# Four modulation vectors as row products on VectorE instead of matmuls on TensorE

## The chip, the cores and the metric

One core of a Trainium2 chip runs the whole program in one launch. The metric is the device time of an execution in microseconds (us), lower is better. Its engines are named as the profile names them: PE (TensorE, matmuls), PEld (its weight loads), DVE (VectorE), ACT (ScalarE), POOL (GpSimd, which here mostly issues DMAs) and SP (SyncE, which issues most loads). Each engine works through its own list of instructions in the order in which the list was built; a wait holds everything behind it on that engine.

## The reference, cut to what matters

Two blocks run one after the other on 512 tokens of width 1024, with 256 context tokens. Block 1 is a mixer of three branches (retention, banded window attention, neighbourhood attention) and a routed FFN. Six vectors of 1024, the modulation, scale and shift its activations:

```python
sc = jax.nn.silu(c)                                    # c: 1024 numbers
mod_x = (sc @ w_mod + b_mod).reshape(-1, 6, d)         # w_mod: 1024 x 6144
hx = modulate(rms_norm(x, g_mix), mod_x[:, 0], mod_x[:, 1])
hc = modulate(rms_norm(ctx, g_mix), mod_c[:, 0], mod_c[:, 1])
mx, mc = hybrid_mixer(hx, hc, w_in, ...)               # retention, window, neighbourhood
x = x + mod_x[:, 2, None] * mx
hx = modulate(rms_norm(x, g_ffn), mod_x[:, 3], mod_x[:, 4])
x = x + mod_x[:, 5, None] * expert_choice_ffn(hx, ...)
```

The first two vectors are needed at once; the last four (`mod_x[:, 2]` to `mod_x[:, 5]`, 4096 numbers out of a 1024 x 4096 matrix, 16 MB) only when the mixer is done. Block 2 (two layers of latent attention, pooled attention and gated linear attention) has modulation vectors of its own for each layer, from the matrices `mw0a`, `mw0b`, `mw1a`, `mw1b`.

## The kernel before

Activations lie transposed, features on the partitions, in tiles of 128 x 512 tokens. A projection streams one 128 x 1024 piece of the weight (`wr`, 512 KB, SP's queue), ACT casts it (`wh`, L395), DVE takes the rest of the split (`wl`, L391), and PE multiplies three products per k-chunk (L404, L405, L406); eight k-chunks fill one PSUM tile `ps`. Three PSUM tiles serve the projections (tag `mm`), so a projection waits until the one three before it has been read.

A modulation vector is computed by `modblock` (L460 to L488): a tile `wm` of 128 x 1024 (512 KB) is loaded on SP's queue into one of `nbig` buffers (tag `wbig`, 3 here), and two matmuls of 512 columns (L471) multiply it with the silu of `c`, spread over 32 columns; the trace counts each as two records. Eight k-chunks accumulate four strips in a PSUM bank; ACT copies them out (L477), four transposes (L480) put them on the partitions, and DVE adds the bias (L486).

`block1_mixer` (L1090) is in stages. Its retention stage (L1111 to L1133) computes two pairs of retention heads: `ret_proj(0)`, `ret_proj(1)` are projections, `ret_attn(0)`, `ret_attn(1)` the attention, with `weave` putting other work between the steps of one. The list `mods` holds four generators: `modblock` for `wmod1` and `wmod2` (16 tiles each, block 1's last four vectors), `mods2` and `mods2g` (`mw1a` and `mw1b`, 24 tiles, block 2's second layer). `pace` (L282) hands out one step of `mods` for so much other work, the numbers of `PACE`. The context's normalised activations `hc` are built in the same stage. The window stage follows: its key is projected, turned by the rope tables `cosw` and `sinw` (lines L721 to L727, DVE; the tables are loaded by POOL), stacked (`kw`, and the context's keys `cw`), then the queries likewise (`qf`, `qw`), and the first scores are L940.

Instructions are listed by a scheduler that orders each engine's list from costs it assumes; what is wrapped in `late` keeps its place in the program's order relative to the others so wrapped and is not moved forward.

Of the kernel before, what the change touches and what calls it, by code (L numbers as in the profile page):

```python
# [7 lines left out]
F32 = mybir.dt.float32  # L8
# [7 lines left out]
D = 1024  # L16
# [127 lines left out]
def prep(i):  # L144
    f = {k: np.asarray(v) for k, v in i.items()}
    o = dict(_constants())
    o["xT"] = _tokT(f["x"][0])
    o["cT"] = _tokT(f["ctx"][0])
    o["cc"] = np.ascontiguousarray(np.stack([_cols(f["c"][0]), _cols(f["c_ctx"])], axis=-1))
    m = _modchunks(f["w_mod"][0])  # L150
    for n, a in enumerate(m):
        o[f"wmod{n}"] = a
    o["bmod"] = _cols(f["b_mod"][0])
    o["gmix"] = _cols(f["g_mix"][0])
    o["gffn"] = _cols(f["g_ffn"][0])
    o["gfin"] = _cols(f["g_final"])
    w = f["w_in"][0]
    off = {}
    at = 0
    for n, s in (("q_r", 512), ("k_r", 512), ("v_r", 512), ("g_r", 512), ("q_w", 512), ("k_w", 128), ("v_w", 128),  # L160
                 ("q_n", 512), ("k_n", 512), ("v_n", 512), ("gates", 3072)):
        off[n] = (at, s)
        at += s
    order = []

    def cols(n, a, m):
        return w[:, off[n][0] + a:off[n][0] + a + m]

    for h in (0, 256):
        order += [_tiles(cols(n, h, 256)) for n in ("q_r", "k_r")]  # L170
        order += [_vtiles(cols("v_r", h, 256)), _tiles(cols("g_r", h, 256))]
    order += [_tiles(cols("k_w", 0, 256)), _tiles(cols("q_w", 0, 512))]
    for h in (0, 256):
        order += [_tiles(np.concatenate([cols("q_n", h, 128), cols("k_n", h, 128)], axis=1)),
                  _vtiles(cols("v_n", h, 256)),
                  _tiles(np.concatenate([cols("q_n", h + 128, 128), cols("k_n", h + 128, 128)], axis=1))]
    order.append(_tiles(cols("gates", 0, 3072)))
    o["win"] = np.concatenate(order)
    o["lgt"] = _bcast(f["ret_decay_logit"][0])
    o["gn"] = _cols(f["ret_gn"][0])  # L180
    o["sink"] = _bcast(f["win_sink"][0])
    o["wbr"] = np.concatenate([_tiles(f["w_ret"][0]), _tiles(f["w_win"][0]), _tiles(f["w_na"][0])])
    o["wout"] = _tiles(f["w_out"][0])
    o["wrt"] = np.concatenate([f["w_router"][0], np.zeros((D, 16), np.float32)], axis=1).reshape(8, 128, 32).transpose(1, 0, 2)

    wg, wu, wd = [f[n][0].reshape(8, 2, 2, 4, 128, 2, 512).transpose(0, 5, 2, 1, 4, 3, 6)
                  for n in ("w_exp_gate", "w_exp_up", "w_exp_down")]
    o["wexp"] = np.concatenate([np.stack([wg, wu], axis=2).reshape(8, 16, 128, 2048), wd.reshape(8, 8, 128, 2048)],
                               axis=1)
    idx, ok = _na_index()  # L190
    rpb = f["na_rpb"][0]
    o["nab"] = np.stack([np.where(g[None], rpb[:, a[0], a[1]], np.float32(NEG)) for a, g in zip(idx, ok)], axis=1)
    _prep2(f, o)
    return {k: np.ascontiguousarray(v) for k, v in o.items()}
# [40 lines left out]
def drain(g):  # L235

    while True:
        try:
            next(g)
        except StopIteration as e:  # L240
            return e.value
# [40 lines left out]
def pace(main, extra, every):  # L282

    due = 0.0
    for c in main:
        yield c
        due += c
        while due >= every:
            due -= every
            c = next(extra, None)  # L290
            if c is not None:
                yield c
# [25 lines left out]
class Kern:  # L318
# [141 lines left out]
    def modblock(s, sc, src, width, dst, bias, col0, big=None, ps=None):  # L460

        nc = s.nc
        ps = s.mm() if ps is None else ps
        nj = width // 512
        for k in range(8):
            for j in range(nj):
                if j % 2 == 0:
                    w = s.wp.tile([128, 1024], F32, name=s.uid("wr"), tag="wraw", bufs=NRAW) if big is None else \
                        big.tile([128, 1024], F32, name=s.uid("wm"), tag="wbig", bufs=s.nbig)
                    nc.sync.dma_start(w, src[k][:, j * 512:j * 512 + 1024])  # L470
                nc.tensor.matmul(ps[32 * j:32 * j + 32, :], sc[:, k, :], w[:, j % 2 * 512:j % 2 * 512 + 512],  # L471
                                 start=k == 0, stop=k == 7)
                if j % 2:
                    yield 0.9
        n = 32 * nj
        rows = s.T(nm="mrow", tag="t5")
        nc.scalar.copy(rows[:n], ps[:n])  # L477
        pt = s.at()
        for i in range(4):
            nc.tensor.transpose(pt[:, i * 128:i * 128 + n], rows[:n, i * 128:i * 128 + 128],  # L480
                                s.const("ident")[:n, :n])
        pv = pt.rearrange("p (i j v) -> p j i v", i=4, j=4)
        for v in range(2):
            o = dst[:, v, col0:col0 + 4 * nj].rearrange("p (j i) -> p j i", j=nj)
            b = bias[:, col0:col0 + 4 * nj].rearrange("p (j i) -> p j i", j=nj)
            nc.vector.tensor_tensor(o, pv[:, 0:nj, :, v], b, ALU.add)  # L486
        yield 0.5


    def rstd_c(s, sq_sum, n, width, fold=None):  # L490
# [599 lines left out]
    def block1_mixer(s, xd, M, ctx2):  # L1090
# [18 lines left out]
        R = [{}, {}]  # L1109
        Y = []  # L1110
        with s.pool("rp") as s.rp, s.pool("mr") as mr:  # L1111
            s.nbig = 3
            pm = s.sc()
            bk = [pm[:, i * 512:i * 512 + 512] for i in range(3)]
            mods = itertools.chain(s.modblock(sc, s.d["wmod1"], 2048, mod, bm, 16, mr, bk[0]),
                                   s.modblock(sc, s.d["wmod2"], 2048, mod, bm, 32, mr, bk[1]),
                                   s.mods2(1, M[1], mr, bk[2]), s.mods2g(1, M[1], mr, bk[0]))
            s.rdl, s.rcos, s.rsin = [s.pconst(s.rp, n) for n in ("dl", "cosr", "sinr")]
            g = s.ret_proj(0, R[0])
            next(g)  # L1120
            c = s.loadx("cT", 256, "pj")
            qc = s.sqsum(c, 256)
            for _ in range(3):
                next(g)
                next(mods)
            s.sc2 = s.silu2("cc2")
            rc = s.rstd_sb(qc, D, 256)
            s.hc = s.normmod(c, 256, A1[:, 1, :], mod[:, 1, 0:8], lambda: s.TT(256, "hc", "hc"), rc)
            drain(pace(g, mods, PACE[0]))
            s.ret_consts()  # L1130
            fill.add(pace(s.ret_proj(1, R[1]), mods, PACE[1]))
            weave(s.ret_attn(0, R[0], Y), fill, 2.4)
            fill.flush()  # L1133
            fill.add(pace(G(0, 10), mods, PACE[2]))
            weave(s.ret_attn(1, R[1], Y), fill, 1.8)
            drain(mods)
# [972 lines left out]
    return {a: b if isinstance(b, (tuple, str)) else (b, w) for a, b in k.items()}  # L2109


PACE = (2, 2.5, 2.5)
NEARLY = 20
NPRE = 44
LATE = True
# [98 lines left out]
```

## Time and profile before

| | before |
|---|---|
| median of 3 runs | 2836.18 us (2832.05 to 2837.74) |
| the profiled execution | 2832.7 us, span 2830.9 us |
| mean granted clock of PE | 0.981 |
| busy share of the span | PE 95%, DVE 55%, ACT 43%, POOL 6% |
| instructions | 41837 |

The profiled execution is 3.5 us under the median; positions in the trace count from the span's start. PE is busy nearly everywhere, with two thinner places among the span's 40 slices. The retention stage with its projections lies at about 38 to 310 us, the first window score at 331 us.

### The profile page before, as it was taken

The page shows a single profiled execution, that of the slowest core. Times are in us where ns is not written, and L with a number is a line of the kernel's source. Part 1 is how long each engine was busy: PE and PEld are TensorE (multiplying, and loading weights), DVE is VectorE, ACT ScalarE, POOL GpSimd, SP SyncE. Part 2 cuts the span into 40 slices and gives each one's busy share as a digit, 9 for nine tenths or more (in the row PEclk, how much of TensorE's full clock was granted, in tenths as well). Part 3 has the DMA queues.
Part 4 walks back from the last instruction along what each step waited for, and adds up shares of the span by engine and source line. Part 5 has one row for each costly group of instructions (what it writes and reads, how often), then busy time and mean ns, then how long its engine had stood idle before and what let it go on. Part 6 is the DMA issues. An engine that isn't in the chain of part 4 may idle for free. (4 is left out here: it accounts for less than half of the span.)

```text
span 2830.9 us, 41837 instructions
## 1 busy us (share of the span) xinstructions
PE 2691.5 (95%) x16372; PEld 1867.8 (66%) x16372; DVE 1567.8 (55%) x2957; ACT 1230.2 (43%) x2159; POOL 159.9 (6%) x260
## 2 busy tenths in 40 slices
PE   6899999999969999999999899999999999999997
PEld 3676677887623555555555477778777677778776
DVE  3554676675442323455222556666876646666874
ACT  3333454453222224455222354455655545555652
POOL 1000001110001000000000100000010000000001
PEclk9999999999979999999999999999999999999999
DMA  8545424635789898888899632214264432214353
GB/s 291 172 171 186 144 82 173 205 112 195 264 332 353 300 339 292 312 295 290 319 336 323 223 123 86 78 43 142 87 203 143 129 127 71 76 38 139 112 174 117
DMA packets 167974, 537.68 MB, mean 190 GB/s; under 512 B 21272, under 2 KB 22376, under 8 KB 167776
## 3 DMA queue, kind: packets, MB, share of 16 engines
q1 hardware_dynamic: 138528, 460.40, 46.6%
q0 software_dynamic: 17152, 52.57, 5.8%
q10 hardware_dynamic: 12096, 22.03, 2.1%
q8 instruction: 129, 2.11, 0.3%
q14 instruction: 69, 0.57, 0.1%
HBM read 484.06 MB, written 48.76 MB: 188 GB/s over the span
## 5 line engine op out<-in xcount | busy, mean ns | idle before, releaser
L391 DVE TENSOR_TENSOR wl<-wr,wh 128x1024 fp32r<-128x1024 f32 x320 | 390.7, 1222 | 358.4 <-ACT wh L395 340.4
L395 ACT CAST wh<-wr 128x1024 fp32r<-128x1024 f32 x320 | 334.1, 1046 | 417.5 <-PE ps L405 324.4
L404 PE MATMUL ps<-hx,wh 128*128 128x512 f32 x1168 | 473.2, 406 | 6.2 <-ACT hx L569 5.5
L405 PE MATMUL ps<-hx,wh 128*128 128x512 f32 x1168 | 468.4, 401 | 0.1
L406 PE MATMUL ps<-hx,wl 128*128 128x512 f32 x1168 | 466.1, 399 | 0.0
L1306 PE MATMUL ps<-we,xe 128*64 128x512 f32 x1024 | 293.5, 609 | 5.5 <-DMA we<-in_wexp 5.0
L404 PEld LDWEIGHTS ps<-hx,wh 128*128 128x128 f32 x1168 | 221.8, 190 | 66.2 <-issue 12.4
L405 PEld LDWEIGHTS ps<-hx,wh 128*128 128x128 f32 x1168 | 221.4, 190 | 51.5 <-issue 8.0
L406 PEld LDWEIGHTS ps<-hx,wl 128*128 128x128 f32 x1168 | 221.3, 189 | 50.0 <-issue 5.0
L673 ACT ACTIVATE P<-ps,st 128x768 f32<-128x768 f32 (+3 forms) x144 | 111.2, 772 | 143.4 <-DVE st L669 108.5
L1306 PEld LDWEIGHTS ps<-we,xe 128*64 128x64 f32 x1024 | 77.9, 137 | 134.1 <-issue 107.1
L404 PE MATMUL ps<-hc,wh 128*128 128x256 f32 x496 | 145.2, 294 | 3.6 <-ACT wh L395 3.4
L406 PE MATMUL ps<-hc,wl 128*128 128x256 f32 x496 | 144.2, 291 | 0.2 <-DVE wl L391 0.2
L1306 PE MATMUL ps<-we,hT 128*64 128x512 f32 x512 | 139.4, 601 | 3.0 <-ACT hT L1346 1.6
L405 PE MATMUL ps<-hc,wh 128*128 128x256 f32 x496 | 140.5, 284 | 0.0
L667 DVE TENSOR_REDUCE st<-ps 128x1 f32<-128x768 f32 (+3 forms) x144 | 114.1, 792 | 41.5 <-PE ps L406 39.0
L695 PE MATMUL ps<-c_ident,P 128*128 128x128 f32 x688 | 109.4, 278 | 5.3 <-ACT PT L698 3.6
L406 PEld LDWEIGHTS ps<-hc,wl 128*128 128x128 f32 x496 | 94.4, 190 | 28.3 <-issue 13.8
L404 PEld LDWEIGHTS ps<-hc,wh 128*128 128x128 f32 x496 | 94.5, 191 | 27.2 <-issue 15.1
L695 PEld LDWEIGHTS ps<-c_ident,P 128*128 128x128 f32 x688 | 79.8, 140 | 40.0 <-ACT PT L698 13.4
L698 ACT COPY PT<-ps 128x512 f32<-128x512 f32 x123 | 70.2, 587 | 77.4 <-PE ps L695 76.7
L471 PE MATMUL ps<-wm,sc_cc 128*32 128x512 f32 x384 | 87.7, 639 | 14.9 <-DMA wm<-in_wmod 14.6
(516 smaller groups left out, 5035.7 us busy)
## 6 DMA issues: line engine op xcount, KB each, us to landing
we<-in_wexp SPq DMA_DIRECT2D x384, 512.0 KB, 7.3
wr<-in_win SPq DMA_DIRECT2D x240, 512.0 KB, 3.9
wm<-in_wmod SPq DMA_DIRECT2D x48, 512.0 KB, 6.4
wr<-in_wbr SPq DMA_DIRECT2D x48, 512.0 KB, 4.4
dram<-th ACTq DMA_DIRECT2D x72, 256.0 KB, 2.2
mth<-dram SPq DMA_DIRECT2D x72, 256.0 KB, 3.1
wr<-in_wout SPq DMA_DIRECT2D x32, 512.0 KB, 3.6
dram<-mth POOLq DMA_DIRECT2D x48, 256.0 KB, 3.1
```

The costliest lines, as they stand in the source:

```text
L391: s.nc.vector.tensor_tensor(out, a, b, ALU.subtract)
L395: i = s.nc.scalar.copy(hi, src)
L404: t.matmul(out, a[0], b[0], start=start, stop=False)
L405: t.matmul(out, a[0], b[1], start=False, stop=False)
L406: t.matmul(out, a[1], b[0], start=False, stop=stop)
L471: nc.tensor.matmul(ps[32 * j:32 * j + 32, :], sc[:, k, :], w[:, j % 2 * 512:j % 2 * 512 + 512], start=k == 0, stop=k == 7)
L667: nc.vector.tensor_reduce(st[:, 0:1], sc[:, :n], AX.X, ALU.max)
L673: nc.scalar.activation(p[:, :n], sc[:, :n], AF.Exp, bias=st[:, 1:2], scale=scale, accum_out=st[:, 2:3])
L695: nc.tensor.transpose(tp[:, j:j + 128], blocks[(i + j) // 128], s.const("ident"))
L698: nc.scalar.copy(parts[i // 512][:, :m], tp[:, :m])
L1306: nc.tensor.matmul(ps[64 * e:64 * e + 64, :], stat[:, k, 64 * e:64 * e + 64], ws[e][:, kk * 512:kk * 512 + 512], start=k == 0, stop=k == 7)
```

## The change

The host prepares the last four column blocks of `w_mod` transposed (`wmodT`: 32 tiles of 128 output rows x 1024) and `c` spread over 128 partitions (`crow`). `silu_row` builds 2 x silu(c) in a 128 x 1024 tile (one load, two ACT tanh, two DVE products). `modrows` then does, 32 times, one load of a 512 KB tile on POOL's queue into one of two buffers, and one DVE instruction that multiplies it with the row and sums along it into one column of `mod`; a single add of the bias ends it. The loads and the products are `late`. `modblock` for `wmod1` and `wmod2` goes, and so do their matmuls, transposes and copies. `nbig` is 2 instead of 3, for the remaining `wm` tiles too. `ret_proj(0)` runs without `mods` beside it, and `mods` is `mods2(1)`, `mods2g(1)`, `modrows`, handed out beside `ret_proj(1)` and `ret_attn(1)`. Line numbers behind the new functions shift by 25 (L721 becomes L746), those ahead by 2 (L391 becomes L393).

```diff
-    for n, a in enumerate(m):
-        o[f"wmod{n}"] = a
+    o["wmod0"] = m[0]
+    o["wmodT"] = f["w_mod"][0][:, 2048:].T.reshape(32, 128, D)
+    o["crow"] = _bcast(f["c"][0])
...
+    def silu_row(s, pool, name):
+        nc = s.nc
+        r = pool.tile([128, D], F32, name=s.uid("row"), tag="row", bufs=1)
+        s.load(r, s.d[name])
+        for h in range(2):
+            x = r[:, h * 512:h * 512 + 512]
+            th = s.T(nm="rth")
+            nc.scalar.activation(th, x, AF.Tanh, scale=0.5)
+            nc.vector.scalar_tensor_tensor(x, th, 1.0, x, ALU.add, ALU.mult)
+        return r
+
+    def modrows(s, row, src, dst, bias, pool):
+        nc = s.nc
+        n = src.shape[0]
+        for t in range(n):
+            w = pool.tile([128, D], F32, name=s.uid("wt"), tag="wbig", bufs=2)
+            s.late(nc.gpsimd.dma_start(w, src[t]))
+            s.late(nc.vector.scalar_tensor_tensor(w, w, 0.5, row, ALU.mult, ALU.mult, accum_out=dst[:, t:t + 1]))
+            yield 0.9
+        nc.vector.tensor_tensor(dst, dst, bias, ALU.add)
...
-            s.nbig = 3
+            s.nbig = 2
-            mods = itertools.chain(s.modblock(sc, s.d["wmod1"], 2048, mod, bm, 16, mr, bk[0]),
-                                   s.modblock(sc, s.d["wmod2"], 2048, mod, bm, 32, mr, bk[1]),
-                                   s.mods2(1, M[1], mr, bk[2]), s.mods2g(1, M[1], mr, bk[0]))
...
             for _ in range(3):
                 next(g)
-                next(mods)
...
-            drain(pace(g, mods, PACE[0]))
             s.ret_consts()
+            drain(g)
+            row = s.silu_row(mr, "crow")
+            mods = itertools.chain(s.mods2(1, M[1], mr, bk[2]), s.mods2g(1, M[1], mr, bk[0]),
+                                   s.modrows(row, s.d["wmodT"], mod[:, 0, 16:48], bm[:, 16:48], mr))
...
-PACE = (2, 2.5, 2.5)
+PACE = (0, 2, 2)
```

DVE's list before, at the end of the retention stage: `ys` and `y` are the last readout, `wl` a weight's split, `mod` and `G` the last of `mods`, `r` the first part of the window key's rope.

```order
L851 TENSOR_TENSOR ys_2109<-ys_2109,gs_1718 128x512
L391 TENSOR_TENSOR y_2122<-ys_2109,y_2122 128x512
L391 TENSOR_TENSOR wl_2350<-wr_2347,wh_2349 128x1024
L486 TENSOR_TENSOR mod_1676<-ps_2185,c_mb_1677 128x8 x2
L1461 TENSOR_TENSOR G_2192<-mod_1676,c_post_2193 128x8 x2
L1144 TENSOR_SCALAR nsink<-c_sink 128x8
L721 TENSOR_TENSOR r_2246<-ps_2220,pc_2202 128x512
L391 TENSOR_TENSOR wl_2388<-wr_2385,wh_2387 128x1024
L725 TENSOR_TENSOR r_2248<-ps_2220,pc_2204 32x512
L726 TENSOR_TENSOR r_2248<-ps_2220,pc_2204 32x512
```

The rope of the window key follows the retention's readout at once. The same place in the list of the changed kernel, a first piece: `wt` are the new tiles, `row` is the silu row.

```order
L393 TENSOR_TENSOR wl_2269<-wr_2266,wh_2268 128x1024
L393 TENSOR_TENSOR y_2061<-ys_2042,y_2061 128x512
L510 SCALAR_TENSOR_TENSOR wt_2104,mod_93<-wt_2104,row_925 128x1024
L393 TENSOR_TENSOR wl_2309<-wr_2306,wh_2308 128x1024
L510 SCALAR_TENSOR_TENSOR wt_2107,mod_93<-wt_2107,row_925 128x1024
L393 TENSOR_TENSOR wl_2347<-wr_2344,wh_2346 128x1024
L510 SCALAR_TENSOR_TENSOR wt_2110,mod_93<-wt_2110,row_925 128x1024
L393 TENSOR_TENSOR wl_2461<-wr_2458,wh_2460 128x1024
L510 SCALAR_TENSOR_TENSOR wt_2113,mod_93<-wt_2113,row_925 128x1024
L510 SCALAR_TENSOR_TENSOR wt_2116,mod_93<-wt_2116,row_925 128x1024
L510 SCALAR_TENSOR_TENSOR wt_2119,mod_93<-wt_2119,row_925 128x1024
L510 SCALAR_TENSOR_TENSOR wt_2122,mod_93<-wt_2122,row_925 128x1024
```

The products stand between the splits `wl`, one for one, and then alone: fourteen in an unbroken run. A second piece, the end of that run (`A`, `m2h` belong to block 1's FFN, `kf` is the window key):

```order
L510 SCALAR_TENSOR_TENSOR wt_2146,mod_93<-wt_2146,row_925 128x1024
L510 SCALAR_TENSOR_TENSOR wt_2149,mod_93<-wt_2149,row_925 128x1024
L510 SCALAR_TENSOR_TENSOR wt_2152,mod_93<-wt_2152,row_925 128x1024
L512 TENSOR_TENSOR mod_93<-mod_93,c_bmod 128x32
L1168 TENSOR_SCALAR nsink<-c_sink 128x8
L1207 SCALAR_TENSOR_TENSOR A_6261<-mod_93,c_gffn 128x8
L1209 TENSOR_SCALAR m2h<-mod_93 128x8
L746 TENSOR_TENSOR r_2205<-ps_2179,pc_2161 128x512
L750 TENSOR_TENSOR r_2207<-ps_2179,pc_2163 32x512
L751 TENSOR_TENSOR r_2207<-ps_2179,pc_2163 32x512
L750 TENSOR_TENSOR r_2207<-ps_2179,pc_2163 32x512
L751 TENSOR_TENSOR r_2207<-ps_2179,pc_2163 32x512
L752 TENSOR_TENSOR kf_2204<-r_2205,r_2207 128x512
```

The rope (now L746) stands behind all 32 products. Eleven of them are in the list before the first instruction of the last retention readout (`ys` at L867), 21 behind it. POOL's list before, where the tables of the retention and of the window are loaded:

```order
L384 DMA pc_290<-in_dl 128x896
L384 DMA pc_292<-in_cosr 128x512
L384 DMA pc_294<-in_sinr 128x512
L384 DMA pc_2202<-in_cosw 128x512
L384 DMA pc_2204<-in_sinw 128x512
L384 DMA pc_2206<-in_tri_l 128x128
L384 DMA pc_2208<-in_tri_r 128x128
```

And in the changed kernel, the last new loads and what follows:

```order
L509 DMA wt_2143<-in_wmodT 128x1024
L509 DMA wt_2146<-in_wmodT 128x1024
L509 DMA wt_2149<-in_wmodT 128x1024
L509 DMA wt_2152<-in_wmodT 128x1024
L386 DMA pc_2161<-in_cosw 128x512
L386 DMA pc_2163<-in_sinw 128x512
L386 DMA pc_2165<-in_tri_l 128x128
L386 DMA pc_2167<-in_tri_r 128x128
```

The loads of the rope's tables moved behind the 32 new loads. PE's list of the changed kernel, in `ret_proj(1)`, where the tiles `wm` of block 2's second layer are used (`hc`, `wh`, `wl` belong to a projection, `qk` to a retention score):

```order
L406 MATMUL ps_1258<-hc_558,wh_1254 128x256
L407 MATMUL ps_1258<-hc_559,wh_1254 128x256
L408 MATMUL ps_1258<-hc_558,wl_1255 128x256
L473 MATMUL ps_289<-wm_1285,sc_cc_499 32x512 x2
L473 MATMUL ps_289<-wm_1330,sc_cc_499 32x512 x2
L473 MATMUL ps_289<-wm_1341,sc_cc_499 32x512
L406 MATMUL ps_1289<-qk_449,qk_491 128x512
L407 MATMUL ps_1289<-qk_450,qk_491 128x512
L408 MATMUL ps_1289<-qk_449,qk_492 128x512
L473 MATMUL ps_289<-wm_1341,sc_cc_499 32x512
L473 MATMUL ps_289<-wm_1384,sc_cc_499 32x512 x2
```

Four tiles of `wm` (1285, 1330, 1341, 1384) are used with no more than one retention score between them, and there are two buffers to load them into; before, such tiles had three.

## Rows read from the trace of the kernel before

**Rows 1.** All engines by stretch; columns: us, then busy us and instructions per engine, clock
```profile
core 0: us, PE busy (x) PEld busy (x) DVE busy (x) ACT busy (x) POOL busy (x), PEclk, DMA share, GB/s
...
75.00:91.00 16.00, 8.51 (x37) 1.73 (x29) 15.88 (x34) 7.83 (x16) 0.00 (x0) 0.93 0.73 260
...
224.00:308.00 84.00, 83.87 (x350) 49.14 (x349) 34.31 (x47) 24.66 (x32) 2.12 (x4) 1.00 0.60 206
...
331.00:782.00 451.00, 447.02 (x2532) 342.12 (x2530) 294.68 (x614) 201.65 (x396) 43.70 (x80) 1.00 0.49 168
```

**Rows 2.** The same view for the tiles `wm` alone: PE, PEld, clock
```profile
91.00:224.00 133.00, 16.55 (x90) 2.56 (x88) 0.98 0.47 160
224.00:290.00 66.00, 10.36 (x56) 1.58 (x56) 1.00 0.55 192
224.00:308.00 84.00, 18.39 (x88) 2.91 (x88) 1.00 0.60 206
```

**Rows 3.** Waits of PE, 40 to 330 us: total, times, longest
```profile
PE ps L471 <- DMA wm<-in_wmod: 10.5, 5, 3.3
```

**Rows 4.** PE's timeline, 48 to 98 us: start, length, instruction, idle before
```profile
48.89 3.92 PE L471 MATMUL ps<-wm,sc_cc 128*32 128x512 f32 x6 [3.26 <-DMA wm<-in_wmod]
52.73 0.80 PE L406 MATMUL ps<-hx,wl 128*128 128x512 f32 x1
...
94.98 0.41 PE L405 MATMUL ps<-hc,wh 128*128 128x256 f32 x1
...
97.11 0.28 PE L406 MATMUL ps<-hc,wl 128*128 128x256 f32 x1
```

**Rows 5.** PE's timeline, the retention's last projection ends; the first window score
```profile
223.87 0.39 PE L406 MATMUL ps<-hx,wl 128*128 128x512 f32 x1
224.19 1.06 PE L471 MATMUL ps<-wm,sc_cc 128*32 128x512 f32 x8
...
331.34 0.50 PE L940 MATMUL ps<-cw,qw 128*128 128x256 f32 x2
```

**Rows 6.** DVE's timeline: first split, last retention readout, window key and query
```profile
47.83 1.22 DVE L391 TENSOR_TENSOR wl<-wr,wh 128x1024 fp32r<-128x1024 f32 x1
...
290.05 0.69 DVE L842 TENSOR_TENSOR ys<-ys,ps 128x512 f32<-128x512 f32 x1 [1.07 <-PE ps L841]
...
308.11 0.68 DVE L721 TENSOR_TENSOR r<-ps,pc 128x512 f32<-128x512 f32 x1
...
311.39 0.68 DVE L725 TENSOR_TENSOR r<-ps,pc 32x512 f32<-32x512 f32 x1
...
314.21 0.69 DVE L727 TENSOR_TENSOR kf<-r,r 128x512 f32<-128x512 f32 x1
...
316.64 2.78 DVE L391 TENSOR_TENSOR kw<-kf,kw 64x512 fp32r<-64x512 f32 x4
319.43 0.85 DVE L391 TENSOR_TENSOR cw<-ps,cw 64x256 fp32r<-64x256 f32 x2
```

**Rows 7.** DVE's groups by shape: count, busy us, mean ns, idle before
```profile
L391 DVE TENSOR_TENSOR wl<-wr,wh 128x1024 fp32r<-128x1024 f32 x320 | 390.7, 1222 | 358.4 <-ACT wh L395 340.4 <-PE ps L837 6.5 <-PE ps L406 5.4
...
L570 DVE SCALAR_TENSOR_TENSOR hx<-nf,mod,hx 128x512 fp32r<-128x512 f32 x24 | 17.9, 744 | 0.0
```

**Rows 8.** DMA issues: count, KB each, median us to landing; two stretches, then whole
```profile
wr<-in_win SPq DMA_DIRECT2D x7, 512.0 KB, 3.2
...
wm<-in_mw1a SPq DMA_DIRECT2D x11, 512.0 KB, 5.1
...
nab<-in_nab POOLq DMA_DIRECT2D x8, 384.0 KB, 3.9
...
pc<-in_sinr POOLq DMA_DIRECT2D x1, 256.0 KB, 6.4
```

**Rows 9.** DVE's timeline, then POOL's, where the window rope's tables are loaded
```profile
258.44 1.15 DVE L772 TENSOR_TENSOR G<-G,gt 128x512 f32<-128x512 f32 x2
...
259.73 0.54 POOL L384 DMA_DIRECT2D pc<-in_cosw  x1 [222.40 <-DVE G L772]
```

## The prediction

> **What bounds the kernel now.** I read the busy shares by stretch first. From 224 to 308 us PE is busy 83.87 of 84 us, while DVE has 34.31; later, from 331 to 782, PE has 447.02 of 451 [rows 1]. So in the stage that the change touches PE is the bound, and DVE has room on average. There is one exception ahead of it: from 75 to 91 PE is busy only 8.51 of 16 us and DVE 15.88 [rows 1]; there DVE builds `hc`. The same view for the `wm` tiles alone shows what modulation costs PE: 18.39 us for 88 records from 224 to 308, 0.209 us each, and 16.55 us between 91 and 224 [rows 2]. The waits of PE say that `wm` transfers are late five times for 10.5 us [rows 3]. Average room on DVE does not settle it, since DVE's list is in order: I then asked what the list puts behind the new products, and that is the window key's rope, on which the first window scores depend.
>
> **What goes.** 32 tiles x 4 records x 0.209 = 26.7 us of PE, and two sets of four transposes. Not all of it is a gain. The 34 or so records before 91 us lie where PE waits anyway: `hc` comes out of DVE at its own pace [rows 1], so taking them away lets PE idle longer. The wait at 48.89 does cost: PE stands 3.26 us for a `wm` tile while the second part of a weight, ready at 47.83 + 1.22 = 49.05, waits behind it until 52.73 [rows 4, 6]. That is 3.3 us off. The price could be a lower clock: with PE thinly used before 91, a 256-column product still takes 0.41 us at 94.98 and 0.28 at 97.11 [rows 4], so a few us at the lower level more would take about 1 back. I leave that out.
>
> From 91 to 224 the old kernel runs 96 records of `wmod1`, `wmod2`; the new one runs some 92 of `mw1a`, `mw1b` in that place, so little changes: about -1 us, a set of transposes included. The gain of matmuls shows after 224: the records that stood there leave.
>
> **What two buffers cost.** `wm` tiles 1285, 1330, 1341 and 1384 are used almost in a row. A tile's load can start only when the one two before it has been used. It lands 3.2 to 5.1 us later [rows 8], while 1 to 1.5 us of PE work lie between. By the list that is 1.8 to 3.7 us for the first, about 1 for the next and 1 to 2 for the last: +4 to +7 us, and I take +4, the low side, since a queue with fewer `wm` loads should land sooner.
>
> So the place that stood at 224.2 [rows 5] comes at T0 = 224.2 - 3.3 - 1 + 4 = 224. Here the last `wm` buffers come free and the first new load can be issued.
>
> **One new product.** No row shows a product that accumulates along 1024 columns. The split `wl` of the same width takes 1.222 us [rows 7]. A scalar_tensor_tensor with two SBUF sources takes 744 ns for 512 columns, and these follow each other closely [rows 7]: twice it less a fixed part is 1.25 to 1.49. The other end is a product at half the pace, twice the split: 2.45. I take 1.25. Nothing makes it cheaper than the split.
>
> **One new load.** 512 KB on POOL's queue is not in this stage. SP's 512 KB take 3.2 us in the quiet stretch after 305 and 5.1 between 225 and 305; POOL's 384 KB take 3.9, POOL's 256 KB in a crowded start 6.4 [rows 8]. I take 3.9: a larger tile than POOL's 384 KB, but in a stretch where loads are few.
>
> The Trainium skill ("DMA: Bandwidth & Descriptors", "Anatomy of one DMA — SWDGE (gpsimd) path") fits a load issued by POOL as 2.0 us + bytes / 436e3, an estimate of 3.2 us for 512 KB. By that page a 384 KB load takes 2.9 us, and the row has 3.9. With 3.2 the sum below would be +15 and not +22.
>
> **The chain of loads and products.** With two buffers a load waits for the product two before it. POOL's load of a table starts 0.14 us after the DVE instruction that frees its tile ends (258.44 + 1.15 = 259.59, start 259.73) [rows 9]. A buffer's cycle is therefore 0.14 + 3.9 + 0.05 + 1.25 = 5.34 us and brings one row; two buffers give one row each 2.67 us, and 32 rows need some 85 us. PE's own work from T0 to the first score, with the `wm` records gone, is (331.3 - 224.2) - 18.4 = 89 us [rows 2, 5]. That would just fit, if the rows ran evenly beside it. They don't, since the list puts them late.
>
> Eleven products stand before the last readout's first instruction (before: 290.05 [rows 6]). That place is 65.9 us behind 224.2, of which 10.36 are `wm` records [rows 2], leaving 55.5; I add 0.9 for the four records that stay and 1.3 for a split or a score held up behind a product whose tile is late. Eleven rows need 29 us, which is hidden: readout at T0 + 57.7. DVE reaches it only then, because it waits for PE there.
>
> From there 21 products are still to come. Two tiles have landed, so 10 cycles and one product: 10 x 5.34 + 1.25 = 54.7 us. The splits and the readout between the first of them lie in the waits for loads. The bias and three small instructions: 0.8. Then the rope and the stacks, in DVE's list without a gap: rope of the key 5 x 0.69 + 0.69, `kw` 2.78, `cw` 2 x 0.86, two splits 2.44, rope of the first query 4.1, part of the second and `qw` 1.4 [rows 6, 7]: 16.6 us. The first score follows at T0 + 57.7 + 54.7 + 0.8 + 16.6 = T0 + 129.8 = 353.8, against 331.34 [rows 5]: **+22.5 us**.
>
> What PE does meanwhile: it still has the projections ahead of the first score, but these fill three PSUM tiles, and the first of them, the window key, is emptied by the rope. PE goes on until these are full and then idles some 30 us. Behind the first score the work is the same as before and PE is 99% busy [rows 1], so the delay isn't won back. The rope's tables, now behind all new loads on POOL's queue, land within the last products' time, or at most 2 to 5 us after; the rope waits for DVE rather than for them, and I cost that at nothing (its price without cover is about 4 us). If the lowered clock after the idle time slows PE, it does so while DVE is still at the rope.
>
> **The sum.** 2832.7 + 22.4 = 2855.1 for an execution like the profiled one; this lay 3.5 us under the median 2836.2, so 2858 on that base. The ends: landing 3.2 makes a cycle of 4.64, 7.0 less over ten cycles, +15; landing 5.1 makes +34; a product of 2.45 adds 1.2 to each cycle, +35; with T0 earlier by 5 (no two-buffer stalls) all move down by 4 to 5.
>
> **Rivals.**
> 1. The loads keep up, and it gets faster. Mechanism: POOL's loads land before DVE is free. Then 21 products take 26.3 us, and the first score is at T0 + 57.7 + 26.3 + 0.8 + 16.6 = 325.4, 6 us early: 2830. It decides where a cycle, of two rows, falls under 3.2 us ((331.3 - T0 - 57.7 - 17.4 - 1.25) / 10 is about 3.1): a landing of at most 1.7 us. For it: 16 DMA engines are loaded lightly after 305. Against: the quietest 512 KB row is 3.2. Cost of being in between: a landing near 1.7 makes no change that a measurement of this kernel can tell (0.2%, 5.7 us); to reach it T0 would have to fall by some 10 us as well as the landing to 3.
> 2. The product is slow. The Trainium skill ("Vector Engine (DVE) Microarchitecture Reference", "Points that are easy to get wrong") says of this instruction with two SBUF sources that aren't bf16 that it "halves throughput". The row at 744 ns for 512 columns, beside 1222 for 1024 [rows 7], isn't halved, but none there accumulates. As a mechanism of this kernel: a product of 2.45, and the sum is +35: 2871.
> 3. POOL's queue is slow: each load takes as long as its slowest single row here, 6.4 [rows 8], because all of it goes through one software queue while SP's `wr` loads run. Cycle 7.84, +47: 2883. For it: 5.4 to 6.4 at the start; against: 3.9 for 384 KB in stages like this.
> 4. The change does not put the products where the list says: no reason, since the list is fixed when the kernel is built.
>
> **Chances.** Forecast (slower, +10 to +36) 66%; rival 1 with a real gain 5%; gain and waits cancel within 0.2% 7%; rival 2 12%; rival 3 10%. The forecast's time is 2858. The likeliest case runs from 2846 to 2872; taking in rival 2 and part of the early-stage gain, the range is 2843 to 2878. Faster 5%, same 7%, slower 88%.
>
> **What would show it.** In the changed profile DVE waits for `wt` transfers, 20 to 30 us in all, near 280 to 340; PE has a hole of about 30 us there whose releaser is DVE's rope of the window key; the first window score is at 345 to 365 us; POOL's new loads come in pairs, 5 us from one use of a buffer to the next; product 1.2 to 1.3 us; PE loses 27 us of busy time in all; later stages are shifted and otherwise alike. The prediction is wrong if DVE's products come without gaps (rival 1), if one takes over 2 us (rival 2), or if PE's hole is at the start of `ret_attn(1)` and not ahead of the window scores.

## The result and the profile after

The changed kernel takes 2870.43 us (median of 4 runs, 2868.97 to 2879.16) against 2836.96 for the kernel before on the same chips: a ratio of 1.0135, 95% interval 1.0117 to 1.0152. It is slower, by some 34 to 38 us; 2858 was forecast, and the range of 2843 to 2878 holds it. The profiled executions have spans of 2868.1 and 2830.9 us, 37.2 apart.

Where in time is it lost? The stretches of the changed kernel, as in [rows 1]: from the first product with `hc` to the first new load, to PE's last projection ahead of the hole, the hole, and all that follows the first window score.

```profile
core 0: us, PE busy (x) PEld busy (x) DVE busy (x) ACT busy (x) POOL busy (x), PEclk, DMA share, GB/s
83.80:229.20 145.40, 139.95 (x741) 100.85 (x741) 76.81 (x133) 51.41 (x77) 0.00 (x1) 0.96 0.43 149
229.20:306.20 77.00, 72.96 (x292) 52.02 (x291) 56.33 (x83) 26.99 (x35) 10.04 (x19) 0.98 0.58 198
306.20:350.20 44.00, 0.00 (x0) 0.00 (x1) 23.53 (x41) 1.53 (x2) 8.98 (x17) 0.54 0.59 206
368.60:2868.00 2499.40, 2389.49 (x14938) 1672.76 (x14937) 1393.12 (x2668) 1111.16 (x1985) 144.50 (x227) 0.98 0.55 189
```

From 306.2 to 350.2 PE does nothing at all, and its granted clock is 0.54 on average, close to the lower of its two levels (half of full speed). From the first window score on, the span has 2499.4 us left; the kernel before has 2830.9 - 331.34 = 2499.6 [rows 5]. So in these two executions the whole loss lies ahead of that score. The waits of PE from 40 to 380 us (total, times, longest) name what it waited for:

```profile
PE ps L406 <- DVE r L751: 44.1, 1, 44.1
PE ps L406 <- ACT hc L594: 7.1, 1, 7.1
PE ps L408 <- DVE wl L393: 6.4, 1, 6.4
PE ps L473 <- DMA wm<-in_mw1a: 4.9, 3, 2.6
PE ps L558 <- DVE rs L533: 3.3, 1, 3.3
```

One wait of 44.1 us on `r` at L751, the window key's rope, which in [rows 3] isn't there. PE's timeline shows its two ends and the first score:

```profile
83.81 0.80 PE L406 MATMUL ps<-hc,wh 128*128 128x256 f32 x2 [7.14 <-ACT hc L594]
...
305.78 0.39 PE L408 MATMUL ps<-hx,wl 128*128 128x512 f32 x1
350.23 0.55 PE L406 MATMUL ps<-hc,wh 128*128 128x256 f32 x1 [44.06 <-DVE r L751]
...
351.86 0.41 PE L406 MATMUL ps<-hc,wh 128*128 128x256 f32 x1
...
368.58 0.50 PE L965 MATMUL ps<-cw,qw 128*128 128x256 f32 x2
```

The first score moved from 331.34 to 368.58, by 37.24 us: all of the difference of the spans. PE's restart runs at the lower level (0.41 us for 256 columns at 351.86, as in [rows 4]). Why the rope was late stands in DVE's timeline: the last readout, three of the products, the rope of key and first query, and `qw`.

```profile
287.33 0.69 DVE L867 TENSOR_TENSOR ys<-ys,ps 128x512 f32<-128x512 f32 x1 [1.98 <-PE ps L866]
...
310.49 1.22 DVE L510 SCALAR_TENSOR_TENSOR wt<-wt,row 128x1024 f32<-128x1024 f32 x1
...
313.22 1.23 DVE L510 SCALAR_TENSOR_TENSOR wt<-wt,row 128x1024 f32<-128x1024 f32 x1 [1.51 <-DMA wt<-in_wmodT]
...
344.95 1.23 DVE L510 SCALAR_TENSOR_TENSOR wt<-wt,row 128x1024 f32<-128x1024 f32 x1 [1.37 <-DMA wt<-in_wmodT]
...
346.60 0.68 DVE L746 TENSOR_TENSOR r<-ps,pc 128x512 f32<-128x512 f32 x1
347.30 0.68 DVE L750 TENSOR_TENSOR r<-ps,pc 32x512 f32<-32x512 f32 x1
...
361.67 0.69 DVE L746 TENSOR_TENSOR r<-ps,pc 128x512 f32<-128x512 f32 x1 [2.54 <-PE ps L408]
...
367.84 1.40 DVE L393 TENSOR_TENSOR qw<-qf,qw 64x512 fp32r<-64x512 f32 x2
```

Between the readout and the rope lie 59 us. From 310.49 to 344.95 fourteen products come 34.46 / 13 = 2.65 us apart, and DVE idles 1.1 to 2.4 us for a load ahead of nearly each of them. The new tiles' own view (duration min/median/max, first and last start, landing):

```profile
L509 POOL DMA_DIRECT2D wt<-in_wmodT x32: 528/528/533, 229.2 to 341.2; - x32
L510 DVE SCALAR_TENSOR_TENSOR wt<-wt,row x32: 1161/1225/1228, 234.1 to 344.9; 128x1024 f32<-128x1024 f32 x32
L510 DVE DVE_READ_ACCUMULATOR wt<-wt,row x32: 80/82/84, 235.2 to 346.1; 128x1 f32 x32
...
DMA to landing us min/median/max: 3.3/3.6/6.6
```

A product takes 1.225 us, and its sum is read by an instruction of its own of 0.08; a load lands in 3.6 (median). POOL's last new load, the rope's sine table behind it, and how long that took to land (us, last column):

```profile
341.20 0.53 POOL L509 DMA_DIRECT2D wt<-in_wmodT  x1 [1.91 <-DVE wt L510]
...
342.26 0.54 POOL L386 DMA_DIRECT2D pc<-in_sinw  x1
...
pc<-in_sinw POOLq DMA_DIRECT2D x1, 256.0 KB, 4.2
```

Issued at 342.26 and landed some 4.2 us later, at 346.5, the table is there 0.8 us ahead of the rope's use of it at 347.30: hidden, but barely.

### The profile page after: what moved, and what is told of

It reads as the page before. It is cut to its first block, busy times and chain, and to the rows that moved or that the text cites. A ratio compares the mean times of both kernels' runs of the same rounds, so it can differ in the third digit from the quotient of the medians.

```text
span 2868.1 us, 41670 instructions
## 1 busy us (share of the span) xinstructions
PE 2666.7 (93%) x16236; PEld 1866.8 (65%) x16236; DVE 1606.6 (56%) x3020; ACT 1228.8 (43%) x2159; POOL 177.7 (6%) x293
## 5 line engine op out<-in xcount | busy, mean ns | idle before, releaser
L393 DVE TENSOR_TENSOR wl<-wr,wh 128x1024 fp32r<-128x1024 f32 x320 | 391.0, 1223 | 325.2 <-ACT wh L397 313.8
L406 PE MATMUL ps<-hc,wh 128*128 128x256 f32 x496 | 145.8, 295 | 55.1 <-DVE r L751 44.1
L406 PEld LDWEIGHTS ps<-hc,wh 128*128 128x128 f32 x496 | 95.6, 193 | 75.8 <-issue 57.1
L408 PEld LDWEIGHTS ps<-hc,wl 128*128 128x128 f32 x496 | 95.8, 193 | 27.5 <-issue 12.2
L407 PEld LDWEIGHTS ps<-hc,wh 128*128 128x128 f32 x496 | 95.6, 193 | 5.6 <-issue 5.1
```

The costliest lines, as they stand in the source:

```text
L393: s.nc.vector.tensor_tensor(out, a, b, ALU.subtract)
L406: t.matmul(out, a[0], b[0], start=start, stop=False)
L407: t.matmul(out, a[0], b[1], start=False, stop=False)
L408: t.matmul(out, a[1], b[0], start=False, stop=stop)
```

## Experiments

Many of the runs below were timed once, and the kernel before alone ranges from 2826.7 to 2845.5 us over its executions. The runs are therefore also compared by one place in the trace that all kernels pass, PE's last neighbourhood score; behind it the traces have between 2154 and 2163 us left. How far this place moves between executions of one kernel wasn't measured, since each was traced once. The kernel before, then the changed one (first and last start before the semicolon):

```profile
L1044 PE MATMUL ps<-cn,qn x64: 277/281/385, 496.3 to 673.4; 128*128 128x256 f32 x64
```

```profile
L1069 PE MATMUL ps<-cn,qn x64: 277/281/383, 533.9 to 711.1; 128*128 128x256 f32 x64
```

It moves from 673.4 to 711.1, +37.7. All experiments but the seventh are edits of the changed kernel.

**Rows first.**

```diff
-            mods = itertools.chain(s.mods2(1, M[1], mr, bk[2]), s.mods2g(1, M[1], mr, bk[0]),
-                                   s.modrows(row, s.d["wmodT"], mod[:, 0, 16:48], bm[:, 16:48], mr))
+            mods = itertools.chain(s.modrows(row, s.d["wmodT"], mod[:, 0, 16:48], bm[:, 16:48], mr),
+                                   s.mods2(1, M[1], mr, bk[2]), s.mods2g(1, M[1], mr, bk[0]))
```

> The three generators of mods are chained in another order: the 32 row products first, block 2's matmuls behind them; loads, queue, two buffers and late are as in the changed kernel, so only the place of the products in the lists moves (from around the last readout to the first half of the retention stage). Theory (the products stand late in an in-order list and, at about 2.6 us a row, hold the window key's rope): no hole ahead of the window scores, the first score some 10 to 20 us earlier than the 331 us of the kernel before, time 2815 to 2828 us. Rival 1 (what costs is the work itself, 85 us of loads and 42 us of DVE, wherever it stands): the hole moves to the first half, 2855 to 2870. Rival 2 (rows delay the splits wl and with them PE, bit by bit): no single hole, waits of PE for wl of 15 us and more, 2835 to 2850.

Measured: 2864.8 us, ratio to before 1.0107 (1.009 to 1.0124); place 702.2 (+28.8). The theory's 2815 to 2828 missed by 37 us. The hole behind the products is gone (PE waits 4.0 us for `r`), but PE's timeline shows what came in its stead:

```profile
316.69 1.05 PE L473 MATMUL ps<-wm,sc_cc 128*32 128x512 f32 x4 [1.45 <-DMA wm<-in_mw1b]
320.35 3.63 PE L473 MATMUL ps<-wm,sc_cc 128*32 128x512 f32 x8 [2.61 <-DMA wm<-in_mw1b]
...
334.13 1.92 PE L473 MATMUL ps<-wm,sc_cc 128*32 128x512 f32 x4 [0.67 <-DMA wm<-in_mw1b]
...
341.43 0.58 PE L406 MATMUL ps<-hc,wh 128*128 128x256 f32 x1 [4.01 <-DVE r L751]
```

Block 2's tiles, now last in `mods`, are left over when the stage's other work has run out. From 314 to 336 us PE has nothing else to do: it waits 8.7 us in all for `wm` loads, two buffers deep, and from 326 us on multiplies at the lower clock (1.92 us for four records, 1.05 at 316.69). The time lies in the first rival's range, but no hole moved to the first half, so neither theory nor rival was right as put: the run doesn't show that rows cost the same anywhere, since something else stood in the bad place. The last experiment repeats it without leftovers.

**Three buffers.** The `bf16` row changes the last four vectors slightly.

```diff
-            s.nbig = 2
+            s.nbig = 3
-            w = pool.tile([128, D], F32, name=s.uid("wt"), tag="wbig", bufs=2)
+            w = pool.tile([128, D], F32, name=s.uid("wt"), tag="wbig", bufs=3)
-        r = pool.tile([128, D], F32, name=s.uid("row"), tag="row", bufs=1)
+        r = pool.tile([128, D], mybir.dt.bfloat16, name=s.uid("row"), tag="row", bufs=1)
```

> Three buffers of 512 KB for the row tiles and for wm instead of two; to make room the silu row is kept in bf16. Places in the lists unchanged. Theory: a cycle of 5.2 us now brings three rows, 1.7 us a row instead of 2.6, so the 21 rows behind the readout take about 36 us instead of 58; with no two-buffer waits of PE (5 us) the time falls by 20 to 27 us, to 2843 to 2850. Rival (DVE's own product time sets the pace): at most 3 us less, 2862 to 2870.

Measured: 2857.8 us, place 693.6 (17.5 earlier than in the changed kernel). PE's hole and the loads' landing (min/median/max):

```profile
PE ps L406 <- DVE r L753: 31.1, 1, 31.1
...
DMA to landing us min/median/max: 3.4/4.6/7.1
```

The hole shrinks from 44.1 to 31.1. The direction is the theory's, but the time is 8 us above its range, as it is 4 below the rival's. The last fourteen products (starting at 296.29 to 327.11) are 30.82 / 13 = 2.37 us apart and not 1.7: with three buffers the median load lands later, 4.6 us in place of 3.6.

**Short product.**

```diff
-            ...(w, w, 0.5, row, ALU.mult, ALU.mult, accum_out=dst[:, t:t + 1])
+            ...(w[:, 0:64], w[:, 0:64], 0.5, row[:, 0:64], ALU.mult, ALU.mult, accum_out=dst[:, t:t + 1])
```

> The product works on 64 of the 1024 columns, so the output leaves out most of each sum; the loads stay whole. Theory: a buffer's cycle loses the 1.1 us of the product, 5.2 becomes 4.1, 21 rows take 43 us instead of 58: 11 to 15 us less, 2854 to 2860. Rival (DVE's product time sets the pace): 21 x 1.15 = 24 us less, near 2845. Rival (loads alone set it, products hidden): no change, 2866 to 2870.

Measured: 2868.9 us, 9 above the theory's range; place 705.1 (6.0 earlier). The product and the landing:

```profile
L510 DVE SCALAR_TENSOR_TENSOR wt<-wt,row x32: 164/225/227, 235.9 to 339.4; 128x64 f32<-128x64 f32 x32
...
DMA to landing us min/median/max: 3.4/4.5/6.5
```

A product lost 1.0 us and the landing gained 0.9. The last fourteen products (305.67 to 339.35) are 33.68 / 13 = 2.59 us apart, 2.65 in the changed kernel. Of the three readings, that the loads alone set the pace comes nearest; the theory's sum of a fixed landing and a product is wrong where loads follow each other this closely.

**Two loads only.**

```diff
+            if t < 2:
                 w = pool.tile([128, D], F32, name=s.uid("wt"), tag="wbig", bufs=2)
                 s.late(nc.gpsimd.dma_start(w, src[t]))
-            ...(w, w, 0.5, row, ...
+            ...(w, w, 0.0, row, ...
```

> Only the first two of the 32 tiles are loaded and all 32 products use these two in turn, with a factor 0, so the output leaves out the matrix product; number and place of the products are as in the changed kernel. Theory: without loads 21 products take 27 us instead of 58, the hole of 44 us shrinks to 10 to 16 us, time 2834 to 2842. Rival (products or rope are what DVE is busy with): less than 10 us gained, 2860 or more. If the rope then waits for its tables, POOL's queue was next in line.

Measured: 2845.0 us, place 688.3 (22.8 earlier, +14.9 to before). PE's hole:

```profile
PE ps L406 <- DVE r L752: 18.1, 1, 18.1
```

Without loads the products run 1.27 us apart at the end, and 18.1 of the 44.1 us of hole remain: the products alone, standing where they stand, still hold up the rope. The time is 3 us above the range: the hole left is longer than the 10 to 16 us that I had given it.

**No rows.**

```diff
-        for t in range(n):
-            ...
+        nc.vector.memset(dst, 0.1)
+        yield 0.9
...
-            row = s.silu_row(mr, "crow")
+            row = None
```

> The changed kernel without the 32 loads and products (their result is a constant, so the output leaves the last four vectors out); matmuls removed and two buffers as in the changed kernel. It shows what removing the matmuls is worth alone. Theory: the hole ahead of the window scores goes; hc stays 7 us earlier, wm between there and the first score falls from 34.9 to 22.4 us, the two-buffer waits cost 5 and other PE work some 4: first score at 318 to 324 us (331 before), time 2817 to 2827. Rival (the removed matmuls lay in PE's waits, nothing is gained): 331 and 2832 or more.

Measured: 2822.0 us, place 661.7 (-11.7 to before). The scheduler orders the gates otherwise here, so the first window score (331.0) isn't comparable, and that part of the expectation can't be read. The place can be used: behind it the span has 2820.2 - 661.7 = 2158.5 us left, 2157.5 in the kernel before. Removing the matmuls, with two buffers for the `wm` tiles that stay, is worth 12 us here, and PE has no hole. By the places of these runs, one trace each, the change of +37.7 is made of -11.7 for the matmuls and the buffer, 14.9 + 11.7 = 26.6 for the products in their place (with the silu row) and 37.7 - 14.9 = 22.8 for their loads.

**Loads on SP's queue.**

```diff
-            s.late(nc.gpsimd.dma_start(w, src[t]))
+            s.late(nc.sync.dma_start(w, src[t]))
```

> The 32 loads are issued by SP, in front of and between the weight loads, instead of by POOL; all else as in the changed kernel. Theory (two loads in flight, each with a fixed part and 512 KB to move, whatever the queue): a row takes 2.3 to 2.7 us as before; since the weight loads wr now stand behind waiting row loads, the last stretch ahead of the window scores is longer: 2865 to 2890. Rival (POOL's software queue is what makes the loads slow): 2.0 us a row or less, 2845 to 2858.

Measured: 2873.1 us, place 712.9. Issue and landing:

```profile
L509 SPq DMA_DIRECT2D wt<-in_wmodT x32: 327/328/328, 230.6 to 341.9; - x32
...
DMA to landing us min/median/max: 3.1/4.3/5.3
```

The last fourteen products (309.29 to 346.36) are 37.07 / 13 = 2.85 us apart, so the rival's 2.0 is excluded: the loads are no faster without POOL's queue.

**The kernel before with two buffers** (`s.nbig = 3` to `2` in the stage).

> The kernel before with two buffers for the wm tiles in place of three, all else unchanged. Theory: PE's waits for wm tiles rise from 10.5 us to 16 to 25; a part lies where PE waits anyhow: 2835 to 2845. Rival (two are as good as three, since a load lands within the work between): 2830 to 2835.

Measured: 2842.0 us beside 2834.8 for the kernel before; place 679.4 (+6.0). The time is in the theory's range, but the kernel before itself ran between 2829.9 and 2845.3 beside it, so only the place speaks. PE's waits for `wm` add up to 11.7 us in place of 10.5, less than the 16 to 25 expected and only a part of the 6 us. PE's busy time grew too, from 2691.5 to 2698.6 us, and from 40 to 91 us its granted clock is 0.77 in place of 0.88: this fits a price paid in part by slower matmuls and not by waits alone.

**Matmuls first.** Block 2's tiles go beside the first projections, the rows behind them; `PACE` is (2, 2, 2).

```diff
+            s.sc2 = s.silu2("cc2")
             g = s.ret_proj(0, R[0])
             next(g)
+            mods = itertools.chain(s.mods2(1, M[1], mr, bk[2]), s.mods2g(1, M[1], mr, bk[0]))
...
                 next(g)
-            s.sc2 = s.silu2("cc2")
+                next(mods)
...
-            drain(g)
             row = s.silu_row(mr, "crow")
-            mods = itertools.chain(s.mods2(1, M[1], mr, bk[2]), s.mods2g(1, M[1], mr, bk[0]),
-                                   s.modrows(row, s.d["wmodT"], mod[:, 0, 16:48], bm[:, 16:48], mr))
+            rows = s.modrows(row, s.d["wmodT"], mod[:, 0, 16:48], bm[:, 16:48], mr)
+            mods = itertools.chain(mods, rows)
+            drain(pace(g, mods, 2))
```

> Block 2's modulation (24 tiles of matmuls) moves into the first projections, where the kernel before had block 1's and where PE waits for hc; the row products follow behind it, from the second projections on, with the same queue, two buffers and late. In DVE's list 28 of 32 products now stand ahead of the last readout, 4 behind it. Theory: no hole ahead of the window scores; wm records behind hc fall from 34.9 to some 15 us; products cost PE bits through A and wl (up to 10 us): first score at 312 to 325 us, time 2812 to 2828. Rival (the rows' chain of 85 us of loads and the products' waits cost PE the same wherever they stand, as where the rows came first): 2850 to 2866.

Measured: 2830.7 us (10 runs), ratio 0.9994 (0.998 to 1.0008): no change from before; the median is 3 us above the range. Place 668.6 (-4.8). No hole is left, but smaller waits of PE for DVE are. The two largest, then the end of the one for `kc` in PE's timeline, and two instructions of DVE around it:

```profile
PE ps L859 <- DVE A L857: 7.4, 5, 3.0
PE ps L406 <- DVE kc L393: 6.8, 1, 6.8
...
183.00 0.58 PE L406 MATMUL ps<-hc,wh 128*128 128x256 f32 x1 [6.85 <-DVE kc L393]
...
174.94 3.35 DVE L874 RECIPROCAL sq<-sq 128x512 f32<-128x512 f32 x1
...
186.70 1.22 DVE L510 SCALAR_TENSOR_TENSOR wt<-wt,row 128x1024 f32<-128x1024 f32 x1
```

Only the waits for `A` can be put down to the products. The one for `kc` ends at 183.0, and DVE runs its first product at 186.7: ahead of `kc` stand the reciprocal of a readout (3.35 us) and a gate's parts.

**Even spread.** As matmuls first, with `PACE` (1.2, 2.6, 2.6) for (2, 2, 2).

> As with matmuls first, but block 2's 24 tiles are handed out one per 1.2 units of work (2 before) and the row products one per 2.6, so that the products start earlier and stand two to a projection, all 32 ahead of the last readout in DVE's list. Theory (what a row costs is DVE's stop behind a load that isn't there yet; two rows to 5.2 us of other work is what the loads can give): PE's waits for A and kc fall from 14 us to under 8, while the denser wm tiles cost 3 to 6 us more in waits of two buffers; 2814 to 2826. Rival (each row costs PE something wherever it stands): 2824 to 2840.

Measured: 2831.3 us (11 runs), ratio 0.9971 (0.9959 to 0.9983): by the ratio 5 to 12 us faster than the kernel before, though the medians are 4.5 apart (2835.8 before) and the place, 671.2, is 2.2 earlier. Beside the changed kernel's median it is 39 us less. That it beats matmuls first, with 2830.7 and a place of 668.6, isn't shown. The wait for `kc` is gone, and those for `A` are 12.2 us:

```profile
PE ps L859 <- DVE A L857: 12.2, 5, 5.9
```

The longest of these, 5.9 us, ends at 193.2 behind a readout and its reciprocal again, and DVE ran no product between 178.5 and 193.7; the rest, 6.3 us, is what products can have cost. `A` and `kc` together fell from 14.2 to 12.2 us and not to under 8, and the time is 5 us above the theory's range and within the rival's. So even well spread the rows may cost PE something; how much is open, since no run has block 2's matmuls first and no rows.

**Not late.** Both `s.late(...)` around load and product taken away.

> Loads and products are no longer held in program order; the scheduler then puts 18 products ahead of the last readout's first instruction and 14 behind it (11 and 21 in the changed kernel). Theory (each product behind the readout costs its 2.6 us of load and product): 7 x 2.6 = 18 us less, 2848 to 2858. Rival (the 32 rows' chain ends when it ends, from the release of the wm buffers on): the last product at 346 as before, 2865 to 2872.

Measured: 2860.5 us, place 697.3 (13.8 earlier). The last product starts at 331.1 in place of 344.95, and the hole is 21.1 us; new waits for `A` (5.6 us in place of 3.0) take a part back. The hole is 23 us shorter, and most of the difference to 13.8 goes into such waits (`wl` too, 9.5 us in place of 6.4). The time is 3 us above the theory's range and 4 below the rival's: products moved ahead of the readout pay off, but at some 2 us each and not at 2.6.

**Half loads.**

```diff
-            s.late(nc.gpsimd.dma_start(w, src[t]))
+            s.late(nc.gpsimd.dma_start(w[:, 0:512], src[t][:, 0:512]))
-            ...(w, w, 0.5, row, ...
+            ...(w[:, 0:512], w[:, 0:512], 0.5, row[:, 0:512], ...
```

> Each row load and product covers 512 of the 1024 columns (256 KB, output leaves out half of each sum). Theory (a cycle is a fixed part, then the transfer, then the product): landing 2.6 to 3.0 in place of 3.6, product 0.75 in place of 1.25, a row takes 1.8 to 2.0 us in place of 2.65: 14 to 18 us less, 2850 to 2857. Rival 1 (the fixed part of a load alone sets it): 2.3 us a row, 2861 to 2866. Rival 2 (throughput alone: half the bytes, half the time): 1.3 us a row, 2838 to 2846.

Measured: 2853.7 us, place 694.5 (16.6 earlier).

```profile
L510 DVE SCALAR_TENSOR_TENSOR wt<-wt,row x32: 632/692/693, 231.6 to 328.1; 128x512 f32<-128x512 f32 x32
...
DMA to landing us min/median/max: 2.9/3.3/4.4
```

Half the bytes land in 3.3 us in place of 3.6, later than the theory's 2.6 to 3.0. The last fourteen products (298.86 to 328.13) are 29.27 / 13 = 2.25 us apart, which is the first rival's number, while the total falls in the theory's range. The first load is issued 2.6 us earlier than in the changed kernel (226.6); what else makes up the difference between pace and total wasn't followed. Throughput alone is excluded.

**Rows first, dense.** As rows first, with `PACE` (0, 1.5, 1.2).

> Rows first again, but mods is handed out faster (one step per 1.5 units beside the second projections, per 1.2 beside the gates, 2 and 2 before), so that no wm tile is left at the end of the retention stage; in the run with rows first, seven of them stood alone there from 314 to 336 us. Theory (what is left of mods at the end of the stage stands alone ahead of the window scores and pays its loads in full): 20 to 24 us less than with rows first, products closer together cost back up to 6 us: 2840 to 2850. Rival (rows cost PE wherever they stand): 2858 to 2868.

Measured: 2847.4 us (9 runs), ratio 1.0045 (1.0027 to 1.0062); place 687.3, 14.9 earlier than with rows first; first score at 340.5 instead of 359.9. The leftover tiles were worth 15 to 19 us, as the theory says. The rival's 2858 is excluded. The run is still 8 to 18 us slower than the kernel before by its interval, and no single wait stands out: PE waits for `wm` (8.4 us), `kc`, `A` and `r` (13 us together).

## Why the prediction was right

The mechanism was the one forecast: 21 products, each behind a load, stand ahead of the rope in DVE's list, and PE runs dry. DVE's waits for `wt` (23.9 us), the hole with the rope as its releaser, the product's 1.225 us, the 24.8 us of busy time that PE lost (2691.5 to 2666.7) and the unchanged rest of the kernel are as the prediction said or near it. The sizes were too small: the hole is 44.1 us and not about 30, the first score at 368.58 is past the 345 to 365 of the prediction, and the time is 12 us above 2858. The first score was forecast at +22.5 us and came at +37.24; four parts of the sum carry the difference.

- T0, forecast 224, is 229.2 (+5.2), the sum of two misses of opposite sign. First, `hc` is first used 7.2 us earlier, and 3.3 were taken off. The prediction has some 34 records before 91 us, in PE's waits; the kernel before has 48 from 40 to 91 us, 14.83 us of PE, and the last of them stood in the way. While ACT wrote `hc` from 86.1 us on, PE waited for two late `wm` tiles:

```profile
40.00:91.00 51.00, 14.83 (x48) 2.03 (x48) 0.88 0.67 229
...
L569 ACT ACTIVATE hc<-nf,mod x8: 492/493/510, 86.1 to 89.2; 128x256 fp32r<-128x256 f32 x8
...
86.61 1.05 PE L471 MATMUL ps<-wm,sc_cc 128*32 128x512 f32 x4 [2.96 <-DMA wm<-in_wmod]
89.12 1.92 PE L471 MATMUL ps<-wm,sc_cc 128*32 128x512 f32 x4 [1.46 <-DMA wm<-in_wmod]
90.97 0.80 PE L404 MATMUL ps<-hc,wh 128*128 128x256 f32 x2
```

Second, from there to T0 the kernel needs 145.4 us in place of 133.2, where 3 more were forecast (4 for two buffers, less 1 for transposes). The two-buffer waits are 4.9 us. The step that failed is to count the records that stay at their old price and the lower clock at nothing (the tiles `wm` alone, changed kernel):

```profile
83.80:229.20 145.40, 21.32 (x92) 2.97 (x92) 0.96 0.43 149
160.00:200.00 40.00, 9.19 (x32) 1.10 (x28) 0.91 0.44 150
...
173.40 1.92 PE L473 MATMUL ps<-wm,sc_cc 128*32 128x512 f32 x2 [2.60 <-DMA wm<-in_mw1a]
```

92 records take 21.3 us of PE, against 16.55 for 90 before [rows 2]. From 160 to 200 us, around two of the three waits for `wm`, the granted clock is 0.91, and 32 records take 9.19 us: behind the wait at 173.40 the records of a tile take 1.92 us, where 1.05 is the rule. That isn't all: from 200 to 229 us, at full clock, 28 records take 7.17 us, and why these cost more no run settles.

- From T0 to the readout 57.7 were forecast, and 287.33 - 229.2 = 58.1 came.
- The 21 rows, forecast 54.7 us, took 346.2 - 287.3 = 58.9 (+4.2). The last fourteen kept the forecast pace of 2.67. The first seven took 310.49 - 287.93 = 22.6 us, 3.2 each: the readout's reciprocal and the splits, which were to lie in the waits for loads, did not wholly fit.
- From the last product to the score 17.4 us were forecast and 368.58 - 346.18 = 22.4 came (+5.0). The step that failed is that DVE's list runs on without a gap and PE's restart is hidden behind the rope. The restart waits for the rope itself: PE began only at 350.23, at the lower level until 353.8, and DVE waited 2.54 us for it at the first query (361.67), besides 2.6 us for ACT's parts of the stacks and of a split. With half the speed for those 3.6 us the clock accounts for an estimated 1.8 of the 2.54 at most; the rest is work that could not start earlier.

Of the rivals, that the loads keep up fell with DVE's waits for them, and the slow product fell with 1.225 us, where a plain split of that shape has 1.222 [rows 7]. The Trainium skill ("Vector Engine (DVE) Microarchitecture Reference", "Points that are easy to get wrong") says of this instruction with two such sources that it "halves throughput"; these rows don't agree. The slow POOL queue fell with a landing of 3.6 us, not 6.4, and with the run on SP's queue, 4.3 us there. By the Trainium skill's fit for loads issued by POOL ("DMA: Bandwidth & Descriptors", "Anatomy of one DMA — SWDGE (gpsimd) path") 512 KB take an estimated 3.2 us. The rows have 3.3 at best, 3.6 in the middle, and 4.5 with the short product.

One rule of the working held only by luck: the row pace as landing plus product, over two. With a shorter product or a third buffer the landing grew and the pace hardly moved (2.59 and 2.37 for 2.05 and 1.7 expected). What the loads in flight share has not been found. Issuing them from SP's queue didn't quicken them, and the transfer's size alone doesn't set the pace. The DMA engines were busy 0.62 of the time during the last products (312 to 344 us), and 0.88 with three buffers (298 to 326), where little room was left.

## What to carry to other kernels

Count what a removed instruction class really occupied on the bounding engine: of 26.7 us of matmuls only some 12 came back. Ahead of `hc`, where records had stood for 14.8 us, PE now waits 16.8 us for `wl`, `rs` and `hc`, and the third buffer that went with them was worth some 6 us to the kernel before. Then look at what stands last in a stage: whatever paced work is left over there, products or matmuls, ran alone ahead of the next stage and paid its loads in full, in the changed kernel and with rows first. Work on an in-order engine that waits for its own loads is best spread at the pace of the loads and ended before the work on which the bounding engine depends: with the rows so placed the kernel took no longer than the one with matmuls (ratios of 0.9994 and 0.9971).

## What the hardware showed beside that

- The sum along the columns costs next to nothing: 1.225 us for the product of 128 x 1024 and 0.08 for reading it out, against 1.222 for a plain split of that shape [rows 7].
- A load's median landing differed with what else was under way: 3.6 us with two row tiles, 4.6 with three, 4.5 with two that follow each other more closely.
- After 44 us without work PE starts at the lower level, 0.41 us for 256 columns (from 351.86 on), and is back at the upper, 0.28, at 353.94.
- A wait can cost PE more than its length: behind one of 2.60 us (173.40) the records of a `wm` tile took 1.92 us in place of 1.05, at the lower level of the clock (0.53 granted from 173.0 to 176.6).
